# A hybrid attention trunk on one core: compression placed behind the second attention group, memsets on POOL, logarithms of pattern counts in per-head tables, minima taken together, Silu where gates are used

## The chip, the cores and the metric

The kernel runs on one core of a Trainium2 chip. The core has five engines with a queue each: TensorE (PE) multiplies matrices, VectorE (DVE) and ScalarE (ACT) work on vectors, GpSimd (POOL) does small work and issues some DMAs, SyncE (SP) issues most of them. An engine takes its own instructions in the order of the program; between engines, semaphores order the work. The metric is the device time of one execution, in microseconds (us), less is better.

## The reference

The reference is one layer: an RMS norm of x (256 tokens, width 4096), one input projection, two attention mixers, and one output projection with the residual and a final norm. All is float32.

```
proj = h @ w_in                 # q_a k_a v_a z_a q_b kc vc ks vs kw vw z_b g_b
o_a  = mixer A: 16 heads, three dilated patterns (128,1) (512,4) (2048,16), causal, ALiBi,
       each pattern a softmax, the three merged by their softmax denominators
o_b  = mixer B: 16 heads in 2 groups; gated sum of three causal branches:
       compressed blocks, selected blocks, window
       kcmp = gelu((blocks(kc) + pe) @ w1) @ w2    (15 blocks of 32 tokens, stride 16)
y    = concat(rmsnorm(o_a) * silu(z_a), rmsnorm(o_b) * silu(z_b)) @ w_out
out  = rmsnorm(x + y)
```

With 256 tokens, the three patterns of mixer A cover keys of the same causal range, so they can be computed as one softmax over all keys in which a key that stands in c patterns counts c times.

## The kernel before

Each float32 operand is split into two parts (`wh` and `wl`, `xh` and `xl`), and a product is three matmuls (`mm3`, L98 to L100). ACT makes the first part (L105), DVE the second one (L106). The two token tiles of 128 rows are `m` = 0 and 1, and a chunk is 512 columns.

The program has five stages. First, a few chunks are streamed. Second, `run_pairs` computes the chunks of q, k, v and qb in pairs, by block products with fewer multiplications. Their partial products are put together in DRAM (`scr_q0` and so on): `put_sums` has ACT copy each PSUM bank into a tile `parts`, and POOL issues a DMA for each place that the bank counts in, a plain write for the first one (L477) and accumulating DMAs for the others (L479). Per pair that is two calls, and the second call of the last pair runs as `rest()` at the head of `begin_rest`, where the third stage begins. Its 15 DMAs carry the name `scr_qb`.

The third stage, the mixers, streams the remaining chunks (the gates z) as `acc` matmuls and mixes tasks in between them. A task is a generator in the deque `tasks`; `run_stream` advances the first task a step for each credit, and credit grows by `pace` = 1.45 with each k step. The order in which the code runs is the order in which each engine's instructions stand. Before, the tasks are: compress k, compress v, the four groups of mixer A (`attend_a`, four heads each), the norm and gates of A, `start_b`, the four groups of mixer B (`attend_b`, two halves each, `attend_half`), the norm and gates of B.

The steps that the change touches:

- `begin_rest` loads `cmat` (784 KB of constants: distances DA and multiplicities MULT for A, distances DB for B) and fetches `kvc` from DRAM.
- `compress` transposes `kc` or `vc` (L812), loads w1 (1024 KB pieces `w`, then split into `w1hl`), multiplies (`ph`, L857 and L858), applies gelu, multiplies by w2, and pads the result with zeros (`kc` memset L890, `wide` memset). Compress v fetches v0 and q0, and each `attend_a` fetches k of its own group (`fetched`) and v and q of the next one; two `fetched` buffers are shared by all.
- In `attend_a`, `scores` computes `s` on PE, and DVE turns it into `n` = slope · DA − s (L667) and takes a minimum per token tile (L671); ACT takes Exp (L673), and DVE multiplies by MULT and sums up the denominators (L674). `turn` transposes `n` (`pt`, L684), `values` multiplies with v (`po`, L696 and L697) and scales by 1/denominator on ACT (L700) and DVE (L701). `pipeline` runs the three a step apart.
- In `attend_half`, `scores` is the like for B (L980, minima L985, Exp with summed denominators L987), `weigh` multiplies by gate and 1/denominator (L993 to L996), and `compressed` builds `c3`, the weights of the compressed blocks in three copies, after a memset (L1012).
- `gate_z` applies Silu to a chunk of gates when it leaves PSUM (L750) and stores it in DRAM where its mixer isn't finished; `gate` multiplies the mixer's output by it (L735).

The fourth stage computes the output projection in pairs; the fifth its last two chunks and the final norm.

Of the kernel before, what the change touches and what calls it, by code (L numbers as in the profile page):

```python
# [18 lines left out]
P = 128  # L19
# [41 lines left out]
N_CONST = 2 * SPAN + N_B0 + N_B + P  # L61


def _constants():
    i = np.arange(P)[:, None]
    blocks = []
    for name in ("da", "mult"):
        for m in range(NT):
            d = (m * P + i) - np.arange((m + 1) * P)[None, :]
            c = ((d >= 0) & (d <= 128)) * 1.0  # L70
            c = c + ((d >= 0) & (d % 4 == 0)) + ((d >= 0) & (d % 16 == 0))
            blocks.append(np.where(c > 0, d, BIG) if name == "da" else c)
    keys = np.arange(P)
    ends = np.where(np.arange(CP) < NC, np.arange(CP) * CST + CBL - 1, 10 * SEQ)
    for m in range(NT):
        cols = [keys, ends, keys] if m == 0 else [P + keys, keys, ends, keys, P + keys]
        d = (m * P + i) - np.concatenate(cols)[None, :]
        blocks.append(np.where(d >= 0, d, BIG))
    blocks.append(np.eye(P))
    return np.concatenate(blocks, 1).astype(np.float32)  # L80
# [3 lines left out]
def hybrid_trunk(ctx: ExitStack, tc: tile.TileContext, a: dict):  # L84
# [496 lines left out]
    def evict_away(key, width=CW, func=AF.Copy, normal=False):  # L581

        def done(ps):
            t = room["ev"].tile([P, NT, width], F32, name="away", tag="ev", bufs=3)
            for m in range(NT):
                nc.scalar.activation(t[:, m], ps[m][:, :width], func, scale=1.0 if normal else rstd[:, m : m + 1])
            nc.sync.dma_start(scratch(key, width), t)
        return done
# [55 lines left out]

    def attend_a(hg):
# [12 lines left out]
        o_tiles("a")  # L658
        parts = [slice(0, P), slice(P, SPAN)]
        live = {}  # L660

        def scores(j):
            s = room["psm"].tile([P, SPAN], F32, name="s", tag="ps")
            mm3(s[:, :P], qh[:, j, :P], ql[:, j, :P], kh[:, j, :P], kl[:, j, :P])
            mm3(s[:, P:], qh[:, j, P:], ql[:, j, P:], kh[:, j], kl[:, j])
            n = room["zq"].tile([P, SPAN], F32, name="n", tag="zt", bufs=4)
            nc.vector.scalar_tensor_tensor(n, K["DA"], SLOPES[hg * 4 + j], s, op0=OP.mult, op1=OP.subtract)  # L667
            mn = room["work"].tile([P, NT], F32, name="mn", tag="mn", bufs=4)
            den = room["work"].tile([P, NT], F32, name="den", tag="den", bufs=4)
            for m in range(NT):  # L670
                nc.vector.tensor_reduce(mn[:, m : m + 1], n[:, parts[m]], axis=AX.X, op=OP.min)  # L671
            for m in range(NT):
                nc.scalar.activation(n[:, parts[m]], n[:, parts[m]], AF.Exp, bias=mn[:, m : m + 1], scale=-1.0)  # L673
                nc.vector.scalar_tensor_tensor(n[:, parts[m]], n[:, parts[m]], 1.0, K["MULT"][:, parts[m]],  # L674
                                               op0=OP.mult, op1=OP.mult, accum_out=den[:, m : m + 1])
            rden = room["work"].tile([P, NT], F32, name="rden", tag="rden", bufs=4)
            nc.vector.reciprocal(rden, den)
            live[j] = (n, rden)

        def turn(j):  # L680
            n, rden = live[j]
            pt = room["psm"].tile([P, SPAN], F32, name="pt", tag="ps")
            for b in range(3):
                nc.tensor.transpose(pt[:, b * P : (b + 1) * P], n[:, b * P : (b + 1) * P], ident)  # L684
            live[j] = (*split_psum(pt, SPAN, "pa"), rden)

        def values(j):
            ph, pl, rden = live.pop(j)
            head = hg * 4 + j

            po = room["pso"].tile([P, NT, 2, HD], F32, name="po", tag="po")
            for m, blocks in enumerate([[(0, 0)], [(P, 0), (2 * P, 1)]]):
                out = po[:, m].rearrange("p s d -> p (s d)")
                for at, b in blocks:
                    vb = v[:, b, j].rearrange("p s d -> p (s d)")
                    nc.tensor.matmul(out, ph[:, at : at + P], vb, start=b == 0, stop=False)  # L696
                    nc.tensor.matmul(out, pl[:, at : at + P], vb, start=False, stop=b == m)  # L697
            for m in range(NT):
                oh = o_at("a", head * HD, HD)[:, m]
# [24 lines left out]
    def gate(which, i, sz=None):  # L724
        r = o_sb["r" + which]
        if sz is None:
# [5 lines left out]
            yield  # L732
        for m in range(NT):
# [12 lines left out]
    def gate_z(which, i):  # L746
        def done(ps):
            sz = [room["zq"].tile([P, CW], F32, name="sz", tag="zt", bufs=4) for m in range(NT)]
            for m in range(NT):
                nc.scalar.activation(sz[m], ps[m], AF.Silu)  # L750
# [53 lines left out]
    def compress(t, which):  # L804

        n = "kv"[which]
# [7 lines left out]
        if which == 1:  # L814
            st["va"], st["qa"] = fetch("v0"), fetch("q0")
        pe = room["work"].tile([P, CBL], F32, name="pe", tag="pe", bufs=2)
# [61 lines left out]
        hh = room["work"].tile([P, 2, 2 * NC], F32R, name="hh", tag="hh", bufs=1)  # L878
        hl = room["work"].tile([P, 2, 2 * NC], F32R, name="hl", tag="hl", bufs=1)
# [4 lines left out]
        if which == 0:  # L884
# [4 lines left out]
            kc = room["work"].tile([P, 2, CP], F32, name="kc", tag="kc", bufs=1)  # L889
            nc.vector.memset(kc, 0.0)  # L890
# [55 lines left out]
    def attend_b(hg):  # L946
# [4 lines left out]
        for _ in range(5):  # L951
            next(first)
            yield
# [7 lines left out]
    def attend_half(hg, m):  # L961
# [8 lines left out]
        n = room["work"].tile([P, 4, N_B], F32, name="nb", tag="n", bufs=2)  # L970
        lo = O_W if m else O_W0
        cuts = [(lo, O_S), (O_S, N_B)] if m else [(lo, O_S + P)]
        sections = [slice(O_S, O_S + (m + 1) * P), slice(lo, O_C)]
        live = {}

        def scores(j):
# [6 lines left out]
            den = room["work"].tile([P, 2], F32, name="den", tag="den", bufs=4)  # L983
            for i, sec in enumerate(sections):
                nc.vector.tensor_reduce(mn[:, i : i + 1], n[:, j, sec], axis=AX.X, op=OP.min)  # L985
            for i, sec in enumerate(sections):
                nc.scalar.activation(n[:, j, sec], n[:, j, sec], AF.Exp, bias=mn[:, i : i + 1], scale=-1.0,  # L987
                                     accum_out=den[:, i : i + 1])
            live[j] = den

        def weigh(j):
            den = live.pop(j)
            nc.vector.reciprocal(den, den)  # L993
            nc.vector.tensor_mul(den, den, gt[:, j, 1:3])
            for i, sec in enumerate(sections):
                nc.vector.tensor_scalar_mul(n[:, j, sec], n[:, j, sec], den[:, i : i + 1])  # L996

        def compressed():
# [5 lines left out]
            nc.vector.tensor_scalar_min(mc, mc, 1.0e30)  # L1004
            nc.vector.tensor_sub(c, mc[:, :, None].to_broadcast(wide), c)
# [5 lines left out]
            c3 = live["c"] = room["work"].tile([P, 4, 3, Q], F32, name="c3", tag="c3", bufs=1)  # L1011
            nc.vector.memset(c3, 0.0)  # L1012
            for i in range(3):
                nc.vector.tensor_mul(c3[:, :, i, :CP], c, dc[:, :, None].to_broadcast(wide))
# [7 lines left out]
        def turn(i):  # L1022
            at, rows, _, vl = blocks[i]
            pt = room["psm"].tile([P, 4, P], F32, name="pt", tag="ps")
            for j in range(4):
                if vl is None:
                    src = live["c"][:, j].rearrange("p i c -> p (i c)")
# [5 lines left out]
            if vl is None:  # L1033

                nc.scalar.activation(h[:rows], flat, AF.Copy)
                nc.vector.tensor_sub(h[2 * Q : rows], flat[2 * Q :], h[2 * Q : rows].bitcast(F32))
# [16 lines left out]
        for j in range(5):  # L1053
            if j < 4:
                scores(j)
            if j > 0:
                weigh(j - 1)
            if j == 4:
                compressed()
# [158 lines left out]
    add_chunk(w_chunk(12), CW, x_lhs, evict_away("za0", func=AF.Silu), pace=pace)  # L1218
# [41 lines left out]
    def begin_rest():  # L1260
# [6 lines left out]
        cmat = room["work"].tile([P, N_CONST - P], F32, name="cmat", bufs=1)  # L1267
        nc.sync.dma_start(cmat, a["consts"][:, : N_CONST - P])
        K["DA"], K["MULT"] = cmat[:, :SPAN], cmat[:, SPAN : 2 * SPAN]
        K["DB"] = [cmat[:, 2 * SPAN : 2 * SPAN + N_B0], cmat[:, 2 * SPAN + N_B0 :]]  # L1270
        t = fetch("kvc")
        tasks.extend([compress(t, 0), compress(t, 1)] + [attend_a(hg) for hg in range(4)] + [mixer_done("a"), start_b()]
# [126 lines left out]
```

## Time and profile before

| | |
|---|---|
| median of 3 runs | 1657.92 us (1657.18 to 1658.92) |
| the profiled execution's own time | 1656.62 us |
| its span in the profile | 1654.8 us |
| mean granted clock of PE | 0.994 |
| third stage (mixers) | from 851.85 us to about 1350 us |

The profile's page gives the busy time of each engine, the same by slices of the span, the DMA queues, the chain of work that ended last, and groups of instructions by line. A row of a group reads: line, engine, operation, tile written and tiles read, shapes, count, then busy us and mean ns, then idle time of the engine just ahead of these instructions and what ended it. A row of a timeline reads: start, duration, engine, line, operation, tiles, count, and in brackets the idle time ahead of it with its releaser. A row of the waits reads: who waited, for whom, us in total, how many times, the longest. Names such as `scr_qb<-parts` say which tile or DRAM area is written from which.

### The profile page before, as it was taken

The page shows a single profiled execution, that of the slowest core. Times are in us where ns is not written, and L with a number is a line of the kernel's source. Part 1 is how long each engine was busy: PE and PEld are TensorE (multiplying, and loading weights), DVE is VectorE, ACT ScalarE, POOL GpSimd, SP SyncE. Part 2 cuts the span into 40 slices and gives each one's busy share as a digit, 9 for nine tenths or more (in the row PEclk, how much of TensorE's full clock was granted, in tenths as well). Part 3 has the DMA queues.
Part 4 walks back from the last instruction along what each step waited for, and adds up shares of the span by engine and source line. Part 5 has one row for each costly group of instructions (what it writes and reads, how often), then busy time and mean ns, then how long its engine had stood idle before and what let it go on. Part 6 is the DMA issues. An engine that isn't in the chain of part 4 may idle for free.

```text
span 1654.8 us, 20979 instructions
## 1 busy us (share of the span) xinstructions
PE 1623.2 (98%) x7772; PEld 1338.6 (81%) x7772; DVE 1354.5 (82%) x1665; ACT 1012.7 (61%) x1291; POOL 138.1 (8%) x183
## 2 busy tenths in 40 slices
PE   9999999999999999999999999999999999999997
PEld 6888978788888888888877787888888878878887
DVE  6586689989898989898966788987866769898984
ACT  6676556665665565656555767676666746656554
POOL 0000000111111111111120000000000000112110
PEclk9999999999999999999999999999999999999999
DMA  9785756979797978887889454544365456798974
GB/s 358 286 317 178 235 200 217 274 245 269 246 270 240 264 254 258 256 258 246 268 294 336 165 205 147 212 140 140 128 211 179 177 200 206 230 271 249 293 284 174
DMA packets 102519, 388.04 MB, mean 234 GB/s; under 512 B 12240, under 2 KB 12880, under 8 KB 88976
## 3 DMA queue, kind: packets, MB, share of 16 engines
q1 hardware_dynamic: 80064, 336.61, 57.6%
q0 software_dynamic: 21920, 49.03, 13.5%
q8 instruction: 61, 1.00, 0.2%
q10 hardware_dynamic: 432, 1.05, 0.2%
q14 instruction: 42, 0.34, 0.1%
HBM read 338.36 MB, written 50.38 MB: 235 GB/s over the span
## 4 chain that ended last, share of the span: by engine, by line
PE 84%; DVE 6%; DMA 3%; issue 3%; ACT 3%; SPq 0%; ACTq 0%; POOLq 0%; POOL 0%; DVEq 0%
PE p L99 14%; PE p L100 13%; PE p L98 13%; PE acc L99 11%; PE acc L100 11%; PE acc L98 10%; PE e L100 2%; PE e L99 2%; PE e L98 2%; DVE bf L459 2%; DMA bw<-in_w_in 1%; DMA w<-in_cmp_v_w 1%; DVE bf L458 1%; DVE bt L452 1%; PE pt L1030 1%
## 5 line engine op out<-in xcount | busy, mean ns | idle before, releaser
L106 DVE TENSOR_TENSOR wl<-w,wh 128x1024 fp32r<-128x1024 f32 (+2 forms) x210 | 246.8, 1178 | 132.0 <-ACT wh L105 131.6
L105 ACT ACTIVATE wh<-w 128x1024 fp32r<-128x1024 f32 (+2 forms) x210 | 214.5, 1024 | 154.6 <-PE acc L100 132.1
L98 PE MATMUL acc<-wh,xh 128*128 128x512 f32 (+2 forms) x768 | 293.8, 383 | 2.6 <-ACT wh L105 2.6
L99 PE MATMUL acc<-wl,xh 128*128 128x512 f32 (+2 forms) x768 | 292.4, 381 | 1.5 <-DVE wl L106 1.5
L100 PE MATMUL acc<-wh,xl 128*128 128x512 f32 (+2 forms) x768 | 291.7, 380 | 0.0
L459 DVE TENSOR_TENSOR bf<-bt,bf 128x2048 fp32r<-128x2048 f32 x99 | 226.1, 2284 | 0.0
L454 ACT ACTIVATE bf<-bt 128x1024 fp32r<-128x1024 f32 x99 | 104.9, 1059 | 170.7 <-DVE bt L452 170.7
L106 DVE TENSOR_TENSOR bp<-bw,bp 128x2048 fp32r<-128x2048 f32 x66 | 151.0, 2288 | 64.8 <-ACT bp L105 64.8
L451 ACT ACTIVATE bf<-bw 128x1536 fp32r<-128x1536 f32 x99 | 147.0, 1485 | 62.4 <-DMA bw<-in_w_in 39.5
L105 ACT ACTIVATE bp<-bw 128x2048 fp32r<-128x2048 f32 x66 | 126.0, 1909 | 78.1 <-PE e L100 63.2
L458 DVE TENSOR_TENSOR bf<-bw,bf 128x1536 fp32r<-128x1536 f32 x99 | 173.3, 1751 | 0.0
L98 PEld LDWEIGHTS acc<-wh,xh 128*128 128x128 f32 x768 | 145.3, 189 | 27.1 <-ACT wh L105 3.8
L99 PEld LDWEIGHTS acc<-wl,xh 128*128 128x128 f32 x768 | 145.4, 189 | 26.7 <-DVE wl L106 3.5
L100 PEld LDWEIGHTS acc<-wh,xl 128*128 128x128 f32 x768 | 145.3, 189 | 24.4
L457 ACT ACTIVATE bf<-bt 128x1024 fp32r<-128x1024 f32 x99 | 105.2, 1063 | 38.7 <-DVE bt L456 37.9
L452 DVE TENSOR_TENSOR bt<-bw 128x1024 f32<-128x1024 f32 x99 | 120.9, 1221 | 9.7 <-DMA bw<-in_w_in 6.5
L99 PE MATMUL p<-bf,sum 128*128 128x512 f32 x288 | 113.2, 393 | 2.9 <-DVE bf L459 2.9
L100 PE MATMUL p<-bf,sum 128*128 128x512 f32 x288 | 112.3, 390 | 0.0
L98 PE MATMUL p<-bf,sum 128*128 128x512 f32 x288 | 112.3, 390 | 0.0
L99 PE MATMUL p<-bp,xh 128*128 128x512 f32 x288 | 112.2, 389 | 0.0
L98 PE MATMUL p<-bp,xh 128*128 128x512 f32 x288 | 112.0, 389 | 0.0
L100 PE MATMUL p<-bp,xl 128*128 128x512 f32 x288 | 112.0, 389 | 0.0
(329 smaller groups left out, 3295.3 us busy)
## 6 DMA issues: line engine op xcount, KB each, us to landing
bw<-in_w_in SPq DMA_DIRECT2D x256, 512.0 KB, 6.1
w<-in_w_in SPq DMA_DIRECT2D x76, 1024.0 KB, 5.0
bw<-in_w_out SPq DMA_DIRECT2D x96, 512.0 KB, 5.1
w<-in_w_out SPq DMA_DIRECT2D x16, 1024.0 KB, 5.0
scr_q<-parts POOLq DMA_DIRECT2D x30, 256.0 KB, 7.3
scr_k<-parts POOLq DMA_DIRECT2D x30, 256.0 KB, 7.7
scr_v<-parts POOLq DMA_DIRECT2D x30, 256.0 KB, 7.7
scr_qb<-parts POOLq DMA_DIRECT2D x30, 256.0 KB, 8.9
```

What stands on the lines that cost most here:

```text
L98: nc.tensor.matmul(out, lh, rh, start=start, stop=False)
L99: nc.tensor.matmul(out, lh, rl, start=False, stop=False)
L100: nc.tensor.matmul(out, ll, rh, start=False, stop=stop)
L105: nc.scalar.activation(h, src, AF.Copy)
L106: nc.vector.tensor_sub(l, src, h.bitcast(F32))
L451: nc.scalar.activation(h[:, :3], w[:, B22:], AF.Copy)
L452: nc.vector.tensor_tensor(t[:, T3 : T1 + 1], w[:, B22 : B11 + 1], w[:, B12 : B12 + 1].to_broadcast([P, 2, CW]), op=OP.subtract)
L454: nc.scalar.activation(h[:, 3:5], t[:, T3 : T1 + 1], AF.Copy)
L457: nc.scalar.activation(h[:, 5:], t[:, T2:], AF.Copy)
L458: nc.vector.tensor_sub(l[:, :3], w[:, B22:], h[:, :3].bitcast(F32))
L459: nc.vector.tensor_sub(l[:, 3:], t, h[:, 3:].bitcast(F32))
L1030: nc.tensor.transpose(pt[:rows, j], src, ident)
```

## The change

The diff does seven things. The order of the tasks is now: A group 0, A group 1, compress k, compress v, A groups 2 and 3, and then as before; `kvc` is fetched in A group 1, and v0 and q0 at the stage's start. The memsets of `kc` and `wide` go to POOL, and `c3` becomes one tile that is zeroed once on POOL at the stage's start. For mixer A, the distance times the slope minus the logarithm of the multiplicity stands in a table of 128 x 384 for each head (192 KB); tables 0 and 1 are asked for at the stage's start, and table h + 2 after the scores of head h, by DMAs on the POOL queue into three buffers. Exp then gives the multiplied weights, and ACT sums the denominators itself. The values of A are copied once for both token tiles, added once, and scaled on ACT. For B one instruction takes both minima, the weights of four heads are computed together, one multiplication weighs both branches, and `c3` takes two copies on ACT and one subtraction. Silu is applied in `gate` (or in `gate_z` where the mixer is finished), and the earlier evictions of z use Copy. `cmat` shrinks to 400 KB.

```diff
+N_TAB = N_B0 + N_B
+N_CONST = N_TAB + NH * SPAN + P
...
+    blocks += [np.where(c > 0, s * d - np.log(np.maximum(c, 1.0)), BIG) for s in SLOPES]
...
+    def load_table(head):
+        if head < NH:
+            tables[head] = room["work"].tile([P, SPAN], F32, name="table", bufs=3)
+            nc.gpsimd.dma_start(tables[head], a["consts"][:, N_TAB + head * SPAN : N_TAB + (head + 1) * SPAN])
...
-        if hg < 3:
+        if hg == 1:
+            st["kvc"] = fetch("kvc")
+        elif hg < 3:
             st["va"], st["qa"] = fetch(f"v{hg + 1}"), fetch(f"q{hg + 1}")
...
-            nc.vector.scalar_tensor_tensor(n, K["DA"], SLOPES[hg * 4 + j], s, op0=OP.mult, op1=OP.subtract)
+            nc.vector.tensor_sub(n, tables.pop(head), s)
+            load_table(head + 2)
...
-                nc.scalar.activation(n[:, parts[m]], n[:, parts[m]], AF.Exp, bias=mn[:, m : m + 1], scale=-1.0)
-                nc.vector.scalar_tensor_tensor(n[:, parts[m]], n[:, parts[m]], 1.0, K["MULT"][:, parts[m]],
-                                               op0=OP.mult, op1=OP.mult, accum_out=den[:, m : m + 1])
+                nc.scalar.activation(n[:, parts[m]], n[:, parts[m]], AF.Exp, bias=mn[:, m : m + 1], scale=-1.0,
+                                     accum_out=den[:, m : m + 1])
...
+            oh = o_at("a", head * HD, HD)
+            nc.scalar.activation(oh, po[:, :, 0], AF.Copy)
+            nc.vector.tensor_add(oh, oh, po[:, :, 1])
             for m in range(NT):
-                nc.scalar.activation(oh, po[:, m, 0], AF.Copy, scale=rden[:, m : m + 1])
-                nc.vector.scalar_tensor_tensor(oh, po[:, m, 1], rden[:, m : m + 1], oh, op0=OP.mult, op1=OP.add)
+                nc.scalar.activation(oh[:, m], oh[:, m], AF.Copy, scale=rden[:, m : m + 1])
...
+            for m in range(NT):
+                nc.scalar.activation(sz[m], sz[m], AF.Silu)
...
-                nc.scalar.activation(sz[m], ps[m], AF.Silu)
+                nc.scalar.activation(sz[m], ps[m], AF.Silu if which in finished else AF.Copy)
...
-            st["va"], st["qa"] = fetch("v0"), fetch("q0")
+            st["va"], st["qa"] = fetch("v2"), fetch("q2")
...
-            nc.vector.memset(kc, 0.0)
+            nc.gpsimd.memset(kc, 0.0)
...
-                nc.vector.memset(wide, 0.0)
+                nc.gpsimd.memset(wide, 0.0)
...
-            for i, sec in enumerate(sections):
-                nc.vector.tensor_reduce(mn[:, i : i + 1], n[:, j, sec], axis=AX.X, op=OP.min)
+            nc.vector.tensor_reduce(mn, branches(j), axis=AX.X, op=OP.min)
...
-            for i, sec in enumerate(sections):
-                nc.vector.tensor_scalar_mul(n[:, j, sec], n[:, j, sec], den[:, i : i + 1])
+            nc.vector.tensor_mul(branches(j), branches(j), den[:, j][:, :, None].to_broadcast([P, 2, size]))
...
-            nc.vector.memset(c3, 0.0)
-            for i in range(3):
-                nc.vector.tensor_mul(c3[:, :, i, :CP], c, dc[:, :, None].to_broadcast(wide))
+            c3 = B["c3"]
+            for i in range(2):
+                nc.scalar.activation(c3[:, :, i, :CP], c, AF.Copy)
+            nc.vector.tensor_sub(c3[:, :, 2, :CP], c, c3[:, :, 0, :CP].bitcast(F32))
...
+        B["c3"] = room["work"].tile([P, 4, 3, Q], F32R, name="c3", bufs=1)
+        nc.gpsimd.memset(B["c3"].bitcast(F32), 0.0)
+        st["va"], st["qa"] = fetch("v0"), fetch("q0")
+        load_table(0)
+        load_table(1)
+        tasks.extend([attend_a(0), attend_a(1), compress(0), compress(1), attend_a(2), attend_a(3), mixer_done("a"), start_b()]
```

The rows below show where the new work stands in the queues. A row has the line, the operation, the tiles and the shape; line numbers of the changed kernel differ by a few from those of before.

POOL's queue at the border of the second and the third stage, before: the last writes into `scr_qb` (the accumulates of `rest()`), and then nothing until the norms of the mixers (`roa`, `rob`).

```order
L479 DMA scr_qb_5824<-parts 128x512
L479 DMA scr_qb_5825<-parts 128x512 x4
L479 DMA scr_qb_5824<-parts 128x512
L479 DMA scr_qb_5825<-parts 128x512 x2
L479 DMA scr_qb_5824<-parts 128x512 x2
L479 DMA scr_qb_5825<-parts 128x512
L115 TENSOR_TENSOR roa<-rsq,nhalf 128x2
L115 TENSOR_TENSOR rob<-rsq,nhalf 128x2
```

The same place of POOL's queue now (`c_5960` is c3):

```order
L478 DMA scr_qb_5824<-parts 128x512
L478 DMA scr_qb_5825<-parts 128x512 x4
L478 DMA scr_qb_5824<-parts 128x512
L478 DMA scr_qb_5825<-parts 128x512 x2
L478 DMA scr_qb_5824<-parts 128x512 x2
L478 DMA scr_qb_5825<-parts 128x512
L1289 MEMSET c_5960 128x384
L649 DMA table<-in_consts 128x384 x11
L902 MEMSET kc 128x32
L908 MEMSET wide 128x192 x2
L649 DMA table<-in_consts 128x384 x5
L114 TENSOR_TENSOR roa<-rsq,nhalf 128x2
```

The memset of c3 and all table loads now stand behind the last accumulate, and the compression's memsets between the loads of tables 10 and 11.

DVE's queue at the start of the third stage, before (`bf` is the last split of the second stage, `wl` are the splits of the streamed weights):

```order
L106 TENSOR_TENSOR bf_1817<-bw_1814,bf_1817 128x2048
L890 MEMSET kc 128x32
L1012 MEMSET c_8020 128x384
L106 TENSOR_TENSOR wl<-w,wh 128x1024 x3
L835 TENSOR_TENSOR bt<-cT,pe 128x480 x2
L106 TENSOR_TENSOR w1hl<-w_5991,w1hl 128x1024
L106 TENSOR_TENSOR wl<-w,wh 128x1024
L106 TENSOR_TENSOR bhl<-bt,bhl 128x32x30
```

And now, down to the first head of A:

```order
L105 TENSOR_TENSOR bf_1817<-bw_1814,bf_1817 128x2048
L105 TENSOR_TENSOR wl<-w,wh 128x1024 x3
L105 TENSOR_TENSOR va<-fetched,va 128x4x128 x2
L105 TENSOR_TENSOR wl<-w,wh 128x1024
L108 SCALAR_TENSOR_TENSOR qaTl<-pt,qaTh 128x512 x2
L105 TENSOR_TENSOR kaT<-pt,kaT 128x512
L105 TENSOR_TENSOR wl<-w,wh 128x1024
L105 TENSOR_TENSOR kaT<-pt,kaT 128x512
L676 TENSOR_TENSOR n<-table,s 128x384
L681 TENSOR_REDUCE mn<-n 128x1 x2
L686 RECIPROCAL rden<-den 128x2
L105 TENSOR_TENSOR wl<-w,wh 128x1024
```

The two memsets are gone from the front, the compression's work is gone from here, and the first subtraction from a table stands with the next weight split behind it.

PE's queue around the first transpose of `n`, now (weight loads left out); before, the compression's matmuls stood in this part of the program:

```order
L99 MATMUL s<-kaT,qaTl 128x256
L97 MATMUL acc<-wh,xh_104 128x512
L98 MATMUL acc<-wl,xh_104 128x512
L99 MATMUL acc<-wh,xl_105 128x512
L97 MATMUL acc<-wh,xh_104 128x512
L98 MATMUL acc<-wl,xh_104 128x512
L99 MATMUL acc<-wh,xl_105 128x512
L97 MATMUL acc<-wh,xh_104 128x512
L693 MATMUL pt<-ident,n 128x128
L97 MATMUL s<-kaT,qaTh 128x128
```

Seven stream matmuls stand between the first head's scores and the transpose of its weights, and the rest of the stream behind that.

More of the change, by code (lines that the diff above doesn't have):

```diff
@@ L66, in _constants @@
     blocks = []
[L67 to L72, printed above, removed]
     keys = np.arange(P)
@@ L78, in _constants @@
         blocks.append(np.where(d >= 0, d, BIG))
+    d = np.concatenate([(m * P + i) - np.arange((m + 1) * P)[None, :] for m in range(NT)], 1)
+    c = ((d >= 0) & (d <= 128)) * 1.0 + ((d >= 0) & (d % 4 == 0)) + ((d >= 0) & (d % 16 == 0))
+    blocks += [np.where(c > 0, s * d - np.log(np.maximum(c, 1.0)), BIG) for s in SLOPES]
     blocks.append(np.eye(P))
@@ L579, in fetch, with evict_away @@
         return t
-    def evict_away(key, width=CW, func=AF.Copy, normal=False):
+    def evict_away(key, width=CW, normal=False):
         def done(ps):
@@ L585, in done @@
             for m in range(NT):
-                nc.scalar.activation(t[:, m], ps[m][:, :width], func, scale=1.0 if normal else rstd[:, m : m + 1])
+                nc.scalar.activation(t[:, m], ps[m][:, :width], AF.Copy, scale=1.0 if normal else rstd[:, m : m + 1])
             nc.sync.dma_start(scratch(key, width), t)
@@ L643, in pipeline @@
             yield
+    tables = {}
+    def load_table(head):
+        if head < NH:
+            tables[head] = room["work"].tile([P, SPAN], F32, name="table", bufs=3)
+            nc.gpsimd.dma_start(tables[head], a["consts"][:, N_TAB + head * SPAN : N_TAB + (head + 1) * SPAN])
     def attend_a(hg):
@@ L802, in open_b, with compress @@
         B["vc3"] = room["work"].tile([3 * Q, 2, HD], F32R, name="vc3", bufs=1)
-    def compress(t, which):
-        n = "kv"[which]
+    def compress(which):
+        n, t = "kv"[which], st["kvc"]
         tT = room["zq"].tile([P, 2, NT, P], F32, name="cT", tag="zt", bufs=4)
@@ L950, in attend_b @@
         first, second = attend_half(hg, 0), attend_half(hg, 1)
-        for _ in range(5):
+        for _ in range(6):
             next(first)
@@ L969, in attend_half, with branches @@
         gt = B["gates"][:, m].rearrange("p (h b) -> p h b", b=3)[:, hg * 4 : hg * 4 + 4]
-        n = room["work"].tile([P, 4, N_B], F32, name="nb", tag="n", bufs=2)
+        n = room["work"].tile([P, 4, 2 * O_S], F32, name="nb", tag="n", bufs=2)
         lo = O_W if m else O_W0
         cuts = [(lo, O_S), (O_S, N_B)] if m else [(lo, O_S + P)]
-        sections = [slice(O_S, O_S + (m + 1) * P), slice(lo, O_C)]
+        size = (m + 1) * P
+        sections = [slice(lo, O_C), slice(O_S, O_S + size)]
+        den = room["work"].tile([P, 4, 2], F32, name="den", tag="denb", bufs=2)
         live = {}
+        def branches(j):
+            return n[:, j, lo : lo + 2 * (O_S - lo)].rearrange("p (s c) -> p s c", s=2)[:, :, :size]
         def scores(j):
@@ L1051, in values @@
                 mm3(live["o"], vh, vl, ph, pl, start=i == 0, stop=i == len(blocks) - 1)
-        for j in range(5):
+        for j in range(6):
             if j < 4:
                 scores(j)
[L1056 to L1059, printed above, removed]
+            else:
+                if j == 4:
+                    gate_weights()
+                for i in range(2):
+                    weigh(2 * (j - 4) + i)
+                if j == 5:
+                    compressed()
             yield
@@ L1217, in hybrid_trunk @@
     add_chunk(w_chunk(21), CW, x_lhs, evict_away("sel"), pace=pace)
-    add_chunk(w_chunk(12), CW, x_lhs, evict_away("za0", func=AF.Silu), pace=pace)
+    add_chunk(w_chunk(12), CW, x_lhs, evict_away("za0"), pace=pace)
     add_chunk([a["w_kw"][g] for g in range(4)], 2 * HD, x_lhs, evict_away("kw", 2 * HD))
@@ L1266, in begin_rest @@
         open_b()
[L1267 to L1272, printed above, removed]
+        cmat = room["work"].tile([P, N_TAB], F32, name="cmat", bufs=1)
+        nc.sync.dma_start(cmat, a["consts"][:, :N_TAB])
+        K["DB"] = [cmat[:, :N_B0], cmat[:, N_B0:]]
+        B["c3"] = room["work"].tile([P, 4, 3, Q], F32R, name="c3", bufs=1)
[4 more added lines that the diff above has]
+        tasks.extend([attend_a(0), attend_a(1), compress(0), compress(1), attend_a(2), attend_a(3), mixer_done("a"), start_b()]
                      + [attend_b(hg) for hg in range(4)] + [mixer_done("b")])
```

30 lines of the change are left out of this document (13 added, 17 removed).

## The prediction

> **What bounds the kernel now.** I read the page's header and busy line first, then the busy time by window around the stage that the change touches, then what TensorE (PE) waited for there, and last the queues of POOL and VectorE (DVE) as timelines.
>
> ```profile
> span 1654.8 us, 20979 instructions
> PE 1623.2 (98%) x7772; PEld 1338.6 (81%) x7772; DVE 1354.5 (82%) x1665; ACT 1012.7 (61%) x1291; POOL 138.1 (8%) x183
> ```
>
> PE is busy for 98% of the span. So a shorter instruction on DVE or ScalarE (ACT) is worth only the PE idle time that it ends, and a new wait of PE costs its full length, because there is almost no slack in which PE could catch up. The stage in question, from the first matmul of the streamed part at 851.85 to about 1350, looks like this. The columns are window, length, busy us of each engine, granted clock, DMA share, GB/s:
>
> ```profile
> 851.00:865.00 14.00, 10.71 (x54) 8.22 (x53) 11.18 (x13) 6.72 (x9) 2.62 (x3) 1.00 1.06 324
> 865.00:890.00 25.00, 23.93 (x133) 19.38 (x132) 15.16 (x20) 12.55 (x16) 4.31 (x5) 1.00 1.06 336
> 896.00:900.00 4.00, 3.93 (x19) 3.74 (x20) 3.15 (x8) 0.06 (x1) 0.00 (x0) 0.61 1.02 426
> 930.00:1035.00 105.00, 103.79 (x570) 84.26 (x569) 85.12 (x215) 76.15 (x145) 0.00 (x0) 1.00 0.50 172
> 1035.00:1210.00 175.00, 174.88 (x916) 142.49 (x916) 145.61 (x421) 122.29 (x267) 0.72 (x1) 1.00 0.44 155
> ```
>
> The attention of group A runs in the fourth window and that of group B behind it. PE is idle for 105.00 − 103.79 = 1.21 us in the one, and for 0.12 us in the next. There is next to nothing to win there, whatever DVE and ACT save. The idle time stands in the first rows, in the compression at the stage's start. These are PE's waits from 851 to 930:
>
> ```profile
> PE ph L857 <- DVE bhl L106: 3.5, 2, 2.9
> PE acc L99 <- DVE wl L106: 1.5, 1, 1.5
> PE ph L858 <- DVE w1hl L106: 1.3, 1, 1.3
> PE ph L857 <- ACT w1hl L105: 1.0, 2, 0.5
> PE pt L610 <- DVE vc L906: 0.6, 1, 0.6
> PE pv L100 <- DVE rl L106: 0.2, 1, 0.2
> ```
>
> **What moving the compression removes.** The first, third, fourth, fifth and sixth of these rows belong to the compression at the stage's start: 3.5 + 1.3 + 1.0 + 0.6 + 0.2 = 6.6 us. They go from this place: −6.6. The longest one, 2.9 us, also pulls the clock down behind it. The chain of work that ended last shows this:
>
> ```profile
> 896.39 0.12 PE ph L858
> ...
> 896.98 0.20 PE ph L857
> ...
> 899.96 0.43 PE acc L98
> ...
> 901.55 0.23 PE acc L98
> ```
>
> From 896.98 to 899.96 + 0.43 = 900.39 steps take 0.20 and 0.43 us, where the same ones took 0.12 before and take 0.23 afterwards: 3.4 us at half speed (the window row 896 to 900 has a granted clock of 0.61), a loss of 1.7. With that wait gone: −1.7.
>
> The second row, 1.5 us, comes from DVE's queue, and the memsets are its cause:
>
> ```profile
> 852.09 0.09 DVE L890 MEMSET kc<- 128x32 f32 x1 [9.23 <-PE e L100]
> 852.21 0.38 DVE L1012 MEMSET c<- 128x384 f32 x1
> 852.50 3.42 DVE L106 TENSOR_TENSOR wl<-w,wh 128x1024 fp32r<-128x1024 f32 x3
> ```
>
> DVE takes its instructions in order. The memset of kc waited 9.23 us for PE's last use of that space, and the weight splits stood behind it. On POOL the memsets hold up no split: −1.5.
>
> **What the tables add.** This is the term that decides. The 16 tables are loaded by the POOL queue, and the first three loads and the memset of c3 stand behind everything that POOL still has to do for the stage before, the 15 writes and accumulates of the last partial products. POOL issues each accumulate only when an earlier one has landed, so this chain runs long into the new stage:
>
> ```profile
> 840.98 2.21 POOL L477 DMA_DIRECT2D scr_qb<-parts  x4 [42.50 <-ACT parts L473]
> ...
> 883.02 0.86 POOL L479 DMA_DIRECT2D scr_qb<-parts  x1 [2.32 <-issue]
> ```
>
> That is 42.0 us from the first write to the issue of the last accumulate. Earlier chains of the same length in the program, first and last rows:
>
> ```profile
> 278.80 2.23 POOL L477 DMA_DIRECT2D scr_q<-parts  x4 [203.35 <-ACT parts L473]
> ...
> 314.99 0.86 POOL L479 DMA_DIRECT2D scr_q<-parts  x1 [1.77 <-issue]
> ...
> 516.42 2.19 POOL L477 DMA_DIRECT2D scr_qb<-parts  x4 [41.42 <-ACT parts L473]
> ...
> 558.88 0.86 POOL L479 DMA_DIRECT2D scr_qb<-parts  x1 [1.72 <-issue]
> ```
>
> They took 36.2 and 42.5 us. I take 39, about the middle, since during the new stall fewer other transfers compete: the last accumulate is issued at 840.98 + 39 = 880.0 (877.2 to 883.5). Then come the accumulate's 0.9 us on POOL, and the first table at 880.9. A POOL memset of c3's size isn't in the trace; DVE's own is 0.38, and I add nothing up to 1 for it and keep it in the range. How long a plain load takes behind an accumulate is in the trace once, near the end of the kernel:
>
> ```profile
> 1545.73 0.87 POOL L479 DMA_DIRECT2D scr_r<-parts  x1 [2.30 <-issue]
> 1546.60 0.58 POOL L491 DMA_DIRECT2D parts<-in_x  x1
> ...
> DMA to landing us min/median/max: 7.2/7.7/8.6
> ```
>
> The loads are of 256 KB, and a table is 192 KB: 7.7, with 7.2 to 8.6 as bounds. The table lands at 888.6. Behind it stand one subtraction, one minimum and one exponential before PE can transpose:
>
> ```profile
> L667 DVE SCALAR_TENSOR_TENSOR n<-cmat,s 128x384 f32<-128x384 f32 x16 | 8.7, 547 | 2.7 <-PE s L100 2.7
> L671 DVE TENSOR_REDUCE mn<-n 128x1 f32<-128x128 f32 x16 | 4.5, 282 | 0.3
> L673 ACT ACTIVATE n<-n,mn 128x128 f32<-128x128 f32 x16 | 6.3, 396 | 6.4 <-DVE mn L671 6.3
> ```
>
> 0.55 + 0.28 + 0.40 = 1.2. So PE may go on at **889.8**.
>
> When does PE come to that transpose? In the new order PE has 37 weight-stream matmuls, 16 transposes and the first six score matmuls ahead of it. Stream steps are 0.23 us apart (the last row of the chain above), and a set of four transposes takes 0.36 to the next step's start:
>
> ```profile
> 855.00 0.60 PE L812 MATMUL pt<-ident,fetched 128*128 128x128 f32 x4
> 855.36 0.47 PE L98 MATMUL acc<-wh,xh 128*128 128x512 f32 x1
> ```
>
> 37 × 0.23 = 8.5, four sets at 0.36 to 0.45 about 1.7, the scores (three of 128x128, three of 128x256, at the spacing of the transposes and half a stream step) 0.85: 11.0 us. From 851.85 that is 862.9. One new wait lies ahead of it: k0's fetch needs the buffer of v0, which is free only when v0 has landed and been split. v0 takes the place on SP that the fetch of kvc has now, and fetches take this long from issue to landing:
>
> ```profile
> 847.12 0.36 SPq L578 DMA_DIRECT2D fetched<-scr_kvc  x1
> ...
> fetched<-scr_k SPq DMA_DIRECT2D x4, 512.0 KB, 3.4
> fetched<-scr_v SPq DMA_DIRECT2D x4, 512.0 KB, 4.8
> ```
>
> v0 is there at about 847.1 + 0.4 + 4.8 = 852.3, its splits on ACT and DVE take some 2 us, and k0 lands at 854.7 + 3.4 = 858.1. PE has the eight transposes of q0 and the stream steps to do until then and would want k0 about 1.6 us sooner (an estimate): +1.6 (0 to 4). PE arrives at 864.5 and stands until 889.8: **+25.3** (from 877.2 + 0.9 + 7.2 + 1.2, that is +22.0, to 883.5 + 0.9 + 1 + 8.6 + 1.2, that is +30.7). Nothing can cover it: PE is in order, and all that it could do, the stream of the next weights, is queued behind the transpose. DVE is stuck as well, since the subtraction that waits for the table has the next weight splits behind it. After such a stop the clock is low for a while, as it was after 2.9 us: +1.7 (0 to 3.4).
>
> The Trainium skill, "DMA: Bandwidth & Descriptors", section "Anatomy of one DMA — SWDGE (gpsimd) path", fits a POOL-issued transfer as about 2.0 us plus its bytes over 436 GB/s. For 192 KB that is 2.45 us, an estimate from this page, against the 7.7 of the row above; by it the sum below would be 5.2 lower. The rows of 7.2 to 8.6 disagree, and the sum goes by the rows.
>
> **Compression in its new place.** Its 128 matmuls aren't fewer, and they still need weight loads and splits. Those share the buffers with the streams, with two of four "o" buffers taken already. Bounds: none of the old waits come back (0), or all of them do (6.6). The old place had DVE full (11.18 of 14.00 us) and DMA saturated (share 1.06); the new one has DMA at half. I take the lower part: +2.5.
>
> **The other edits.** Per head the A side loses two multiplications with accumulation on DVE and gains two accumulator reads on ACT; beside it the row of ACT's table loads at the gates:
>
> ```profile
> L674 DVE SCALAR_TENSOR_TENSOR n<-n,cmat 128x256 f32<-128x256 f32 x16 | 6.7, 421 | 0.6
> L674 DVE SCALAR_TENSOR_TENSOR n<-n,cmat 128x128 f32<-128x128 f32 x16 | 4.6, 288 | 3.9 <-ACT n L673 3.4
> L750 ACT ACT_TABLE_LOAD x8 | 10.3, 1283 | 0.1
> ```
>
> DVE saves 6.7 + 4.6 = 11.3 us. ACT gains 32 short reads and loses ten of its loads of function tables at 1.283 (Silu no longer alternates with Copy and Exp there). The values of A and the weights and minima of B lose small operations on the same two engines. All of this lies beside a PE that idles 1.21 + 0.12 us in these windows. The gain is at most that: −1.3. Bounds: 0, and −3, if as much again is hidden in the modelled ends of matmuls. If the cover were gone, that is, if DVE were the bound, it would be the 11.3 us and more; at 85.12 of 105 us it isn't. Later tables are asked for two heads ahead, some 13 us at 105/16 = 6.6 us a head, more than 7.7: 0.
>
> **The sum**, against the profiled execution's own 1656.62 us (1.3 below the median of the runs shown, 1657.92, so the median should stand as much higher): −6.6 − 1.7 − 1.5 + 1.6 + 25.3 + 1.7 + 2.5 − 1.3 = +20.0, that is 1676.6. I say **1677**.
>
> **The rivals.**
> - *The first table comes in time* (faster). If the chain ended early, the terms 25.3 and 1.7 would go: −7.0, about 1650. The point from which this decides: at a stop of 25.3 − 20.0 = 5.3 us the sum is zero, so the table would have to land before 868.6, the last accumulate be issued before 860, 19 us after the chain's start. For it: fewer loads compete early in the stage. Against it: no chain took under 36.2. Chance 0.04.
> - *The load is short once it is issued* (the page's fit, as a mechanism: the load runs beside the last accumulates instead of behind them). The table would land 2 to 3 us after its issue, 5 sooner: about 1671.5. Against it are the rows of 7.2 to 8.6. Chance 0.14.
> - *The compression stalls as much as before, and the chain takes its old 42 us.* 4.1 + 3.0 more: about 1684. For it: w1 is read through fewer buffers. Chance 0.12.
> - *The change does nothing that counts*: PE covers it all, the first table isn't waited for because the order of the queues is of no effect. 1656.6. Against it: both PE and DVE take instructions in order in every timeline read. Chance 0.03.
>
> **How the numbers follow.** The forecast has 0.67. A measurement of this kernel can tell about 0.2% from no change, 3.3 us; forecast, short load and stalling compression are all far on the slower side, 0.93. The range leaves out the first and the last rival and the tails of the terms: from 1666 (a short load and the short chain, 1671.5 − 2.8, and k0 without its wait, −1.6, and some more) to 1687 (the late bounds, 1676.6 + 5.4, and half the compression's upper end with k0's).
>
> **What the changed profile would show.** Right: PE has one wait of 20 to 30 us near 865, at the first transpose of n (its releaser an Exp or the table's DMA), with DVE's subtraction idle for as long, waiting for the table; POOL's last scr_qb accumulate at 877 to 884 and the first table load right behind; a half-clocked stretch of some 3.4 us after it; no such wait at the other 15 tables; PE's idle time in the A and B windows still about 1 us. Wrong: a first table issued before 860, a landing under 4 us, a PE wait under 10 us at this place, or waits for tables all along group A.

## The result and the profile after

The changed kernel takes 1675.72 us (median of 4 runs, 1672.55 to 1678.61) against 1657.55 us before: a ratio of 1.0108, 95% interval [1.0088, 1.0128]. It is slower by 18 us. The profiled execution is the fastest of the four, 1672.55 us with a span of 1670.8.

The page's span and busy times (engine, busy us, share of the span, instructions):

```profile
span 1670.8 us, 20883 instructions
PE 1625.5 (97%) x7772; PEld 1340.3 (80%) x7772; DVE 1330.9 (80%) x1446; ACT 1016.3 (61%) x1355; POOL 148.0 (9%) x203
```

DVE has 219 instructions and 23.6 us less to do than before, and the kernel is longer all the same: PE's busy time has hardly moved, so what has come is idle time of PE.

The waits of PE in the changed kernel from 851 to 935 (who waited, for whom, us in total, how many times, the longest):

```profile
PE pt L693 <- ACT n L683: 11.0, 1, 11.0
PE pt L609 <- DMA fetched<-scr_k: 4.1, 1, 4.1
```

All the waits that stood in this stretch before are gone, and two have come. The longest one, at the first transpose of `n`, names ACT's Exp. But that is only the last link. The chain of work that ended last, in this stretch, goes further back:

```profile
849.74 10.91 DMA scr_qb<-parts
...
862.17 6.28 DMA scr_qb<-parts
...
872.62 0.85 POOL scr_qb L478
...
874.47 0.45 POOL c L1289
874.91 5.10 DMA table<-in_consts
880.07 0.41 issue
880.48 0.57 DVE n L676
881.07 0.30 DVE mn L681
881.39 0.50 ACT n L683 x2
881.93 0.48 PE pt L693
```

The accumulates into `scr_qb`, the memset of c3, the load of the first table, the subtraction, the minimum, the Exp, the transpose: one after the other, with nothing of PE among them from 849.74 to 881.93. POOL's and DVE's timelines show the same from the engines' side (the bracket is the idle time ahead, with its releaser):

```profile
841.86 2.20 POOL L476 DMA_DIRECT2D scr_qb<-parts  x4 [41.51 <-ACT parts L472]
...
873.92 0.86 POOL L478 DMA_DIRECT2D scr_qb<-parts  x1 [0.45 <-issue]
874.47 0.75 POOL L1289 MEMSET c<- 128x384 f32 x1
874.91 1.91 POOL L649 DMA_DIRECT2D table<-in_consts  x3
```

```profile
867.96 0.69 DVE L105 TENSOR_TENSOR kaT<-pt,kaT 128x512 fp32r<-128x512 f32 x1
880.48 0.56 DVE L676 TENSOR_TENSOR n<-table,s 128x384 f32<-128x384 f32 x1 [11.84 <-DMA table<-in_consts]
...
883.35 1.23 DVE L105 TENSOR_TENSOR wl<-w,wh 128x1024 fp32r<-128x1024 f32 x1 [0.78 <-ACT wh L104]
```

DVE stands for 11.84 us with the next weight split behind it. The windows around it, and the two windows of groups A and B (window, length, busy us of PE, PEld, DVE, ACT, POOL, granted clock, DMA share, GB/s):

```profile
862.00:868.00 6.00, 5.99 (x18) 4.96 (x19) 1.88 (x3) 2.14 (x3) 2.33 (x3) 0.51 1.07 303
866.00:882.00 16.00, 4.98 (x23) 3.92 (x22) 2.99 (x5) 1.88 (x5) 6.93 (x10) 0.71 0.93 190
881.00:886.00 5.00, 4.07 (x17) 3.65 (x18) 3.42 (x9) 2.45 (x7) 0.69 (x2) 0.60 0.26 59
935.00:1050.00 115.00, 112.48 (x617) 90.07 (x617) 84.82 (x142) 79.16 (x153) 4.06 (x9) 1.00 0.67 240
1060.00:1225.00 165.00, 163.04 (x841) 132.45 (x840) 121.95 (x257) 109.71 (x256) 0.00 (x0) 1.00 0.41 143
```

PE looks busy in the first of them, but its clock is granted at 0.51: after each of the two waits it runs at half speed for some us. In the window of group A, which now holds the compression too, PE is idle for 2.52 us, and in that of group B for 1.96; the windows of A and B before had 1.21 and 0.12. Its waits from 1050 to 1365:

```profile
PE pt L1090 <- ACT oT L1086: 1.0, 1, 1.0
PE pt L609 <- DMA fetched<-scr_qb: 0.7, 1, 0.7
PE acc L98 <- DVE wl L105: 0.6, 1, 0.6
```

### The profile page after: what moved, and what is told of

Its sections match the earlier page's. It is cut to its first block, busy times and chain, and to the rows that moved or that the text cites. A ratio compares the mean times of both kernels' runs of the same rounds, so it can differ in the third digit from the quotient of the medians.

```text
span 1670.8 us, 20883 instructions
## 1 busy us (share of the span) xinstructions
PE 1625.5 (97%) x7772; PEld 1340.3 (80%) x7772; DVE 1330.9 (80%) x1446; ACT 1016.3 (61%) x1355; POOL 148.0 (9%) x203
## 4 chain that ended last, share of the span: by engine, by line
PE 86%; DVE 6%; DMA 3%; issue 3%; ACT 2%; POOL 0%; ACTq 0%; POOLq 0%; SPq 0%; DVEq 0%
PE p L98 14%; PE p L99 14%; PE p L97 14%; PE acc L98 11%; PE acc L99 10%; PE acc L97 10%; PE e L99 2%; PE e L97 2%; PE e L98 2%; DVE bf L458 2%; DMA scr_qb<-parts 1%; DMA w<-in_w_in 1%; PE pt L1047 1%; DVE bf L457 1%; DVE bt L451 1%
```

## The experiments

The theory: 14 of the 18 us come from one place in a queue, the first table behind POOL's accumulates. The rivals: the tables cost by themselves; the compression's new place costs; the edits of groups A and B cost. Each ratio below is to the kernel before, with its 95% interval.

**Tables on SP's queue.**

```diff
-            nc.gpsimd.dma_start(tables[head], ...)
+            nc.sync.dma_start(tables[head], ...)
```

> The changed kernel, with the 16 table loads issued on SP's queue in place of POOL's, and nothing else. If the cost of the change is that the first table stands behind POOL's chain of accumulates: the stop of PE at the first transpose of n (11.0 us in the profile of the changed kernel) is gone, with the half-clocked 0.8 us behind it; the wait for k0 (4.1) and its half clock (2.2) stay. Time 1659 to 1664. If the tables cost by their traffic, or if it is the other edits that cost: 1673 to 1678, as the changed kernel.

Measured: 1662.42 us, 1.0024 [1.0013, 1.0036]. PE's waits from 851 to 930 are now

```profile
PE pt L609 <- DMA fetched<-scr_k: 4.9, 1, 4.9
PE ph L869 <- DVE bhl L105: 0.7, 1, 0.7
PE pt L609 <- DMA fetched<-scr_q: 0.2, 1, 0.2
```

The stop at the first transpose is gone, and 1.0108 − 1.0024 = 0.84% with it, 14 us. The tables' bytes are the same, so their traffic isn't what costs.

**The compression first again, tables left on POOL.** The task list and the fetches of kvc, v0 and q0 as before, the rest as changed.

```diff
-        tasks.extend([attend_a(0), attend_a(1), compress(0), compress(1), attend_a(2), attend_a(3), ...
+        tasks.extend([compress(0), compress(1), attend_a(0), attend_a(1), attend_a(2), attend_a(3), ...
```

> The changed kernel, with the compression ahead of the first attention group again, and kvc, v0 and q0 fetched where they were before; the tables stay on POOL's queue. If only the tables' place behind the chain costs, and not the tables: the first table is there some 40 us before its first use, no wait for it and none for k0. The compression's old waits come back (6 to 7 us), the wait of 1.5 for the memsets doesn't, group B keeps its new waits of some 3 us. Time 1656 to 1661. If the tables or the other edits cost by themselves: 1670 or more.

Measured: 1659.85 us, 1.0014 [1.0002, 1.0027]. The first table is issued at 886.54 here, later than in the changed kernel, and nobody waits for it: what PE waits for up to 935 is the compression (bhl 4.0 us, hh 2.4, vc 0.5). So tables on POOL without the new order don't make the loss, and by the run with the tables on SP, the new order without them on POOL doesn't either. It takes both.

**The move alone.** The kernel before with the compression moved in the same way, no other edit.

> The kernel before, with the compression alone moved behind the second attention group (kvc fetched there, v0 and q0 at the stage's start); multiplicities, memsets and group B as before. By the theory of the chain the move itself is about even: 7 us of waits at the start go, the wait for k0 (4.1) with its half clock (2.2) and 2 us of the compression in its new place come. Time 1655 to 1660. If the place is what costs: 1668 or more.

Measured: 1658.93 us, 1.0008 [0.9998, 1.0019]. About even, as expected: the compression's waits at the start go, and 4.2 us for k0 come. Beside that, PE waits 1.2 us for group B's first fetch (`scr_qb`), and from 1050 to 1240, in group B:

```profile
PE po L98 <- ACT pbh L105: 1.6, 1, 1.6
PE acc L99 <- DVE wl L106: 0.2, 1, 0.2
PE pt L1032 <- DVE c L1016: 0.2, 1, 0.2
```

The kernel before has no wait at these places, and the code of groups A and B is the old one here. So the new order alone brings some 3.2 us of waits to group B.

**A dose on POOL's queue.**

```diff
-        nc.gpsimd.memset(B["c3"].bitcast(F32), 0.0)
+        for _ in range(21):
+            nc.gpsimd.memset(B["c3"].bitcast(F32), 0.0)
```

> The changed kernel, with the memset of c3 on POOL done 21 times in place of once, ahead of the first table's load; nothing else is computed otherwise. A dose on POOL's queue alone. By the theory of the chain the first table comes 20 x 0.44 to 0.75 = 9 to 15 us later, and PE's stop at the first transpose of n grows by as much: 1685 to 1691, a stop of 20 to 30 us. If PE's delay doesn't hang on POOL's queue: 1673 to 1679.

Measured: 1680.88 us, 1.0135 [1.0116, 1.0154]. POOL's timeline and the first line of PE's waits from 851 to 940:

```profile
874.99 0.86 POOL L478 DMA_DIRECT2D scr_qb<-parts  x1 [1.01 <-issue]
875.52 10.25 POOL L1290 MEMSET c<- 128x384 f32 x21
885.72 1.69 POOL L649 DMA_DIRECT2D table<-in_consts  x3
```

```profile
PE pt L693 <- ACT n L683: 19.2, 1, 19.2
```

PE's stop grows from 11.0 to 19.2 us by work on POOL alone: the tile that it clears isn't read before group B. The direction is as forecast, the size under it, and the time lies between the two forecasts: the table is issued 885.72 − 874.91 = 10.8 us later, but lands quicker (its subtraction begins 3.1 us after the issue, 888.82 against 885.72, where it was 880.48 − 874.91 = 5.6). By then the accumulates and all other loads have drained: the DMA share is 0.00 from 880 to 885 here, and was 0.98 from 874 to 880 in the changed kernel.

**k0 before v0, tables on POOL.** For the first group k0 is fetched at the stage's start, v0 once q0 is transposed, and v0's split stands behind the first scores.

```diff
-        st["va"], st["qa"] = fetch("v0"), fetch("q0")
+        st["qa"], st["va"] = fetch("q0"), fetch("k0")
...
+        if not hg:
+            vsrc = fetch("v0")
         yield from transposed(ksrc, "ka")
...
+            if j == 0 and hg == 0:
+                v = split_values(vsrc)
```

> The changed kernel with k0 fetched before v0 in the same way, and the tables left on POOL's queue. By the theory of the chain the table's landing alone sets when PE goes on: PE comes to the first transpose some 6 us sooner and waits as much longer (16 to 18 us where it was 11), and the time stays at 1673 to 1678. If the two waits add up: the stop stays near 11 and the time falls to 1667 to 1670.

Measured: 1677.36 us, 1.0113 [1.0097, 1.0129]. PE's one wait from 851 to 930:

```profile
PE pt L702 <- ACT n L689: 19.7, 1, 19.7
```

The wait for k0 is gone, and the time hasn't moved: PE comes earlier and waits longer for the same table. The two waits don't add up; the table's landing sets when PE goes on.

**k0 before v0, tables on SP.** The same edit with the tables on SP's queue.

> The changed kernel with the tables on SP's queue, and for the first attention group k0 fetched at the stage's start in place of v0; v0 is fetched once q0 is transposed, and split behind the first head's scores. If the rest of the loss is the wait for k0 (4.9 us there) and its half clock (some 2): no wait for k0, time 1654 to 1657. If that wait only moves (to v0's split, to the first values): 1659 to 1664.

Measured: 1659.44 us, 1.0013 [1.0003, 1.0023], 3 us under the run with the tables on SP alone, where 5 to 8 were expected. The time is in the second forecast: most of the wait only moved. The first values now wait 2.0 us for `pah`, which stands on ACT behind the late split of v0, then 0.5 for `pal`, and PE waits 2.2 us for k1. Half of the 3 us stands elsewhere, at group B's first fetch, where the wait falls from 2.3 to 0.8.

**Group B as before, tables on SP.** `attend_half` is that of the kernel before, with its memset of c3 on POOL.

> The changed kernel with the tables on SP's queue, and group B's half (minima, weights, compressed branch, c3 made anew for each half, its memset on POOL) as in the kernel before. If the new waits of PE in the first half of group B (oT 1.2, wl 0.8, nb 0.3, pbh 0.3 us) come from taking the four heads' weights together: they go, and the time is 2 to 3.5 us under that with the tables on SP's queue alone, 1659 to 1660.5. If they come from where the work of the gates now falls: they stay, 1661.5 to 1664.

Measured: 1662.80 us, 1.0022 [1.0012, 1.0031]. The wait for oT (1.0 us with the tables on SP alone) goes, as the theory of the heads taken together has it, but one for `wh` comes in its place, and the time doesn't move. PE's waits from 1050 to 1365:

```profile
PE p L98 <- DVE bf L457: 1.5, 1, 1.5
PE acc L97 <- ACT wh L104: 0.9, 1, 0.9
PE acc L98 <- DVE wl L105: 0.8, 1, 0.8
```

The first of these rows belongs to the fourth stage and stands with the tables on SP alone too. So B's edits aren't what costs there, as the move alone has shown from the other side. That theory falls.

**All three together.** Tables on SP, k0 before v0, group B as before.

> All three together: tables on SP's queue, k0 fetched before v0, group B's half as before. If the three account for the loss, what is left is what the move of the compression and the memsets on POOL bring: 1650 to 1655, a ratio of 0.996 to 0.998 to the kernel before. If something else costs as well: 1657 or more.

Measured: 1660.19 us, 1.0014 [1.0004, 1.0024]. The upper branch: something else costs as well. Part of it is the k0 wait itself, which has moved again: its profile has 2.9 us of PE waiting for `pah`, behind v0's late split.

**The move, made clean.** The kernel before (no tables, A, B and gates as before), the compression moved, memsets on POOL, and v0 in a free buffer of another pool, so that k0 waits for nobody.

```diff
+        st["va"] = room["o"].tile([P, NT, CW], F32, name="fetched", tag="o", bufs=4)
+        st["qa"], st["k0"] = fetch("q0"), fetch("k0")
+        nc.sync.dma_start(st["va"], scratch("v0"))
...
-        ksrc = fetch(f"k{hg}")
+        ksrc = fetch(f"k{hg}") if hg else st.pop("k0")
```

> The kernel before, with the compression moved behind the second attention group, all its memsets on POOL, and q0, k0 and v0 all fetched at the stage's start, v0 into a free buffer of the o pool so that k0 needn't wait for it. No tables, and group A, group B and the gates as before. If the move's own gain (7 us of waits, 1.7 of half clock) was only eaten up by the wait for k0 and the memsets' 1.5: no wait for k0, no early wait for wl, 1650 to 1654, a ratio of 0.995 to 0.998. If what is gained at the stage's start comes back later in the stage: 1656 to 1659.

Measured: 1656.75 us, 0.9995 [0.9984, 1.0006]. In the second branch, and no gain that can be told. Group B's new waits of the move alone stand here too (qb 1.2, pbh 1.6), and PE's waits from 851 to 930 show one that neither branch named:

```profile
PE pt L610 <- DVE qaTl L109: 3.1, 1, 3.1
PE ph L859 <- DVE bhl L106: 0.5, 1, 0.5
PE pt L686 <- DVE n L676: 0.2, 1, 0.2
```

v0 is now the third fetch on SP and lands at 858.5; ACT and DVE, in order, stand at its split with q0's split behind it.

**The whole change, made clean.** The changed kernel with the tables on SP and v0 in that buffer.

> The changed kernel with the tables on SP's queue and v0 in a free buffer of the o pool, so neither the table nor k0 is waited for; all other edits of the change as they are. If the other edits lie beside a full PE: within 2 us of the kernel without tables and with old groups A and B, 1650 to 1656. If the gates' Silu or taking the heads together costs PE time in group B: 2 to 5 us above that one.

Measured: 1660.85 us, 1.0018 [1.0008, 1.0028], 0.23% or 4.1 us above the run before it, which lacks the edits of groups A and B, the tables and the late Silu. These edits are at best worth nothing here. Its profile shows waits that the run before it hasn't, 3.4 us for k1, 1.0 for oT and 0.6 for wl, but that one has 1.6 for pbh and 1.3 more for q0's split instead. These rows make only part of the 4.1 us, and which edit costs wasn't taken apart.

**The memsets alone.**

```diff
-            nc.vector.memset(kc, 0.0)
+            nc.gpsimd.memset(kc, 0.0)
...
-                nc.vector.memset(wide, 0.0)
+                nc.gpsimd.memset(wide, 0.0)
...
-            nc.vector.memset(c3, 0.0)
+            nc.gpsimd.memset(c3, 0.0)
```

> The kernel before, with the memsets of kc, wide and c3 on POOL and nothing else. PE's wait of 1.5 us for wl at the stage's start goes: 1655.5 to 1657, a ratio of 0.999. If POOL's accumulates, which now have two memsets among them that wait for PE's last use of that space, run later and matter: 1658 or more.

Measured: 1655.28 us, 0.9991 [0.9980, 1.0001]. PE's early wait for wl is gone from its profile. The size fits 1.5 us, but the interval reaches 1.

**The clean move with v0 split later.** As the clean move, with v0's split behind the transposes of k0.

```diff
-        v = split_values(vsrc)
+        v = split_values(vsrc) if hg else None
...
         yield from transposed(ksrc, "ka")
+        if not hg:
+            v = split_values(vsrc)
```

> The kernel with the compression moved, the memsets on POOL and v0 in a free buffer, as in the run before it, and v0's split placed behind the transposes of k0, so that DVE and ACT don't stand waiting for v0 ahead of q0's split. If PE's wait of 3.1 us for q0's split there is all that held the move back: it goes, and the time is 1652 to 1655, a ratio of 0.997 to 0.999. If the wait only moves to the first head's scores or to its values: 1656 to 1658.

Measured: 1653.34 us, **0.9973 [0.9964, 0.9983]**: faster than both kernels. PE's waits from 851 to 930:

```profile
PE pt L610 <- DMA fetched<-scr_k: 1.1, 1, 1.1
PE ph L861 <- DVE bhl L106: 0.5, 1, 0.5
```

The first row is k1 now, at 888. 1.6 us is left in this stretch of the 8.1 that stood in it before.

## Why the prediction came out

The sign, the place and the mechanism were right, and 1677 stands beside 1675.72. But the terms were not as right as their sum. Each against the changed kernel's profile, in us:

| term | forecast | measured | from |
|---|---|---|---|
| wait for the memsets | −1.5 | −1.5 | no such row; the memsets alone on POOL give 0.9991 |
| compression's waits at the start, and their half clock | −6.6 − 1.7 | −6.6 − 1.7 | no such rows from 851 to 935 |
| wait for k0 | +1.6 | +4.1 | the wait row |
| half clock behind it | 0 | about +2.8 | 0.51 granted from 862 to 868; two sets of four transposes and six stream steps take 3.47 and 2.98 us, where the set before them took 1.84 |
| wait for the first table | +25.3 | +11.0 | the wait row |
| half clock behind it | +1.7 | about +1.4 | steps of 0.43 us for 0.23 at 884.03, 884.46, 0.34 at 884.88 (0.5); transposes and scores ahead of them 1.90 us, 1.00 at the next head (0.9) |
| compression in its new place | +2.5 | +1.8 | bhl 1.3 and vc 0.5 in the waits from 935 to 1050 |
| groups A and B | −1.3 | about +2.3 | qb 0.7, oT 1.0, wl 0.6 |

The measured column gives +13.6; the profiled execution is 15.9 above the one before. Of the rest, 0.9 lies ahead of the stage (its first stream step is at 852.72 where it was at 851.85), and 1.4 us stand in no row.

**The table's wait was mis-sized, from both ends.** PE came later than 864.5, at 870.9, through the stage's later start, the k0 wait and its half clock. (k0's fetch took 6.6 us from its issue at 855.39, where the prediction took the row's 3.4; and it put nothing for a half clock there, with no reason given, though its own trace showed one behind a stop of 2.9 us.) And the table came sooner than 888.6, at 874.91 + 5.10 = 880.0. The step that failed is "I take 39": the chain took 873.92 − 841.86 = 32.1 us. The bounds of 36.2 to 42.5 came from chains that ran beside other loads. With the compression first the chain is 42.0 (before) and 885.54 − 842.55 = 43.0 us long; with attention first it was 32.1 here, 33.4 under the dose and 34.0 with the move alone, but 37.6 in the whole change made clean and 40.6 with v0 split later. So the place of the compression alone doesn't set it. The last two have no long stop of PE, and the stream's loads go on: in the run with v0 split later the DMA engines moved 335 and 316 GB/s from 858 to 874 and from 874 to 884, in the changed kernel 283 and 137. That fits the prediction's own reason, that fewer transfers compete during the stop, with an effect larger than it took; it wasn't tried by itself, and what sets the length stays open.

The landing was mis-sized as well: 5.1 in the chain of work, under the bound of 7.2. The Trainium skill's fit that the prediction cites ("DMA: Bandwidth & Descriptors", section "Anatomy of one DMA — SWDGE (gpsimd) path") gives 2.45, an estimate from that page. Under the dose, with the DMA engines idle, the chain of work has 2.66 for the same load, near that estimate; behind the accumulates it was twice as long.

**That the sum held is in part luck.** The table's wait is 14 us under its term, and the k0 wait, its half clock and groups A and B make up for 2.5 + 2.8 + 3.6 = 8.9 of them. The profiled execution is also 3.2 us under the median. Of the signs that were named, the stop of 11.0 us isn't one of 20 to 30, the last accumulate at 873.92 is ahead of 877 to 884, and PE's idle time in the windows of A and B is 2.52 and 1.96, not about 1. What was no luck is that the waits for k0 and for the table trade against each other: PE goes on when the table lands, however early it comes, and taking the first wait away left the time at 1677.36.

**The rivals.** The table in time: it was not, and only with the tables on SP does that case come about. It was forecast at about 1650 and gave 1662.42: the k0 wait is 4.9 us there, a half clock follows it, and group B's waits come to 3.9 (qb 2.3, oT 1.0, wl 0.6). The short load: the landing lay between the two, 5.1. The compression stalling as before: no, 1.8. The change that does nothing: that nearly holds for the two parts. The move alone (1.0008) and the other edits with the old order (1.0014, with 1.0002 as the lower end of its interval) each came out near 1.

**Wrong outright** was groups A and B at −1.3, "the gain is at most that". The bound was right for the gain, but a loss was left out. PE's waits in group B, from its first fetch on, are 2.3 us here and none before. With the move alone, so with the old code of A and B, they are 3.2; with the new code and the compression first they are 1.6 (qb 1.0, wl 0.4, oT 0.2). So either of the two brings waits, and that taking heads and minima together is the cause isn't shown: with group B's old code oT's wait left, and the time stayed the same. How the new order makes group B wait stays open. What is left of the 0.24% with the tables on SP is in part the k0 wait (0.11% by the run with k0 first); the rest isn't settled among the new order, the tables on SP, the late Silu and the values of A.

## What to carry to other kernels

In these runs a load that was put on a queue stood behind everything that this queue still had to do for the stage before, though the code asks for it at the stage's start. So before a load goes on a queue for its being idle "on average" (POOL was busy for 8% of the span), look at what is queued there at the moment when the first load is needed. Two edits that are nearly harmless alone can cost together: with the compression first, the first table was asked for 43 us ahead of its first use (886.54 and 929.28), until the same change took away the compression that stood there. And the waits that start this stage gave way only when both the first fetches and the first splits were put in order, as the 0.27% of the last run shows.

## What the runs showed of the hardware that wasn't expected

- The half clock behind a stop of PE doesn't grow with the stop. Behind 4.1 us PE ran at half speed for 6.0 us (0.51 granted from 862 to 868), which cost some 2.8 us; behind 11.0 us for 3.0 us; behind 19.2 us (the dose) for 5.7. A stop of 2.2 us (k1, in the run with k0 before v0 and the tables on SP) had a stretch of 3.4 us behind it that began 1.4 us late, while those of 3.1 us (the move, made clean) and 3.4 us (the whole change, made clean) had none: 1.00 granted.
- A memset of 128x384 on POOL takes 10.25 / 21 = 0.49 us in a row of 21 and 0.75 alone, against 0.38 on DVE before.
- The same load on the POOL queue landed 2.66 us after its issue with the DMA engines idle, and 5.10 behind accumulates.
